# The attention's weights split during the first MLP, kept in DRAM, and a new order in the weight queue

## The chip, the cores and the metric

The kernel runs on one core of one Trainium2 chip. A core has five engines that work side by side, each through its own list of instructions in order: TensorE (PE in the profile) multiplies matrices, VectorE (DVE), ScalarE (ACT) and GpSimd (POOL) work element by element, and SyncE (SP) issues the transfers between DRAM and the on-chip memory SBUF. TensorE writes its sums into PSUM, from which DVE and ACT read them. An engine that waits for another one's result holds up everything behind it in its own list.

The metric is the device time of one execution in microseconds (us), the median of several runs.

## The reference, cut to what matters

The model has two layers over 512 tokens of 1024 numbers. The first layer mixes tokens with pooled averages; the second is a causal "stick-breaking" attention with 16 heads. Each is followed by an MLP with 4096 hidden values and a squared ReLU, and everything stands between root-mean-square norms.

```python
def sq_relu_mlp(h, w_up, w_down):
    u = jnp.matmul(h, w_up)
    return jnp.matmul(jnp.square(jax.nn.relu(u)), w_down)

for layer in range(DEPTH):
    h = rms_norm(x, mix_pre_g[layer])
    if layer < N_A:
        m = pool_mixer(h, pool_w[layer], pool_scale[layer])
    else:
        q = jnp.matmul(h, w_q[j])...
        o = stick_breaking_attention(q, k, v)
        m = jnp.matmul(o..., w_o[j])
    x = x + rms_norm(m, mix_post_g[layer])
    h = rms_norm(x, mlp_pre_g[layer])
    x = x + rms_norm(sq_relu_mlp(h, w_up[layer], w_down[layer]), mlp_post_g[layer])
    if layer == N_A - 1:
        kv = jnp.matmul(rms_norm(x, kv_norm_g), w_kv)
```

Inputs and output are float32. The gains of the norms ahead of the key, value and query projections can be multiplied into the weights' rows.

## The kernel before

**Products in three parts.** Every float32 product is made of three matmuls of a shorter type, fp32r. Each operand is split into a high part (a cast on ACT) and a low part (the rest after subtracting the high part, on DVE); the product is high x high + high x low + low x high. `mm3` (L217 to L219) and `up_block` (L555 to L557) issue such triples. `split` (L196, L197) does the two steps for activations, `weight` (L115) for weights: it loads a raw weight of 128x1024 numbers (512 KB) into one of two raw buffers, multiplies gains into it on POOL where the weight has any (two instructions at L138), casts it (L126) and subtracts (L128). Four of the first MLP's weights are subtracted on POOL, all others on DVE.

**The weight queue.** `queue` lists all weights that are split whole, in the order of use: for each layer the 32 column blocks of the up matrix (`up`) and the last four row blocks of the down matrix (`dn`), and ahead of the second layer's the 32 weights of the attention (8 `v`, 8 `k`, 8 `q` with gains, 8 `o` without). `fill` takes weights off its head as long as fewer than four are made and not yet used, `get` takes one out for use. The split weights lie in four slots, each with a high and a low tile. The `dn` weights have a place of their own (`dn_pool`), which exists only towards the end of an MLP, when buffers of the groups come free; `fill` stops at a `dn` weight until then. The first attention weights stand behind the four `dn` weights of the first MLP.

**The MLP.** 28 of the 32 hidden blocks are worked in five groups (of 2, 3, 3, 3 and 3 pairs) by a scheme that replaces eight block products by seven (class `Seven`). A group has seven products, each with a left operand (tile `a`, sums of squared activations, made on POOL at L417 and split at L196, L197) and a right operand (tile `w`, sums of blocks of the down matrix, made on DVE at L436 and split). The two halves of a group's down rows are loaded at L401, the second half into the tile `xn`. The operands are made two products ahead. Between the products stand the up products of the next group: 24 matmuls each, then ReLU and square on ACT. A product and an up product make one period. The first group starts when the first four up products are done. TensorE's part of a product is at L462, and its result is added to the tiles `y` at L471. After the groups, the last four hidden blocks are contracted plainly with the `dn` weights (`contract`); there the output's norm (`Update`: squares at L200, gains at L242, statistics at L206 and L213, the residual at L248, the next norm at L280) and its transposes for the next stage (L289) run along.

**Attention.** Sixteen heads in eight pairs run through a pipeline written out by hand (`ATT_ORDER`): values (V), keys and queries (K, P), scores and weights (S), transposes (T), mixing (A), output projections (O, E). `fill` is called in between.

**What sets the order.** The program text gives an order, and a scheduler that estimates when each instruction could run moves instructions within each engine's list, SP's among them, before the kernel is built. On the chip each list is then worked strictly in order. Buffers are named by tags: a new tile of a tag waits until the old tile's last reader is done. `grow` and `spare` are two such buffers of 512 KB, which hold rows of gains.

Of the kernel before, what the change touches and what calls it, by code (L numbers as in the profile page):

```python
# [10 lines left out]
F32 = mybir.dt.float32  # L11
# [4 lines left out]
P = 128  # L16
D = 1024
# [47 lines left out]
def trunk(ctx, tc, x, consts, gcol, grow, pw, wup, wdn, wq, wk, wv, wo, out):  # L65
# [3 lines left out]
    work = pool("work")  # L69
    wts = pool("wts")  # L70
    psum = pool("psum", 8, space=bass.MemoryType.PSUM)

    nc.scalar.preload_act_table_set("sigmoid_and_others")

# [74 lines left out]
    def place(k):  # L149

        if k[0] == "dn":
            return dn_pool[0].pop(0)
        if k == ("o", 6):
            both = att_pool[0].tile([P, 2, D], F32R, tag="v", bufs=2, name=name("w"))
            return [both[:, 0], both[:, 1]]
        if k == ("o", 7):
            return [att_pool[0].tile([P, NSEG], F32R, tag="w", bufs=2, name=name(x))[:, :D] for x in "hl"]
        return [wts.tile([P, D], F32R, tag=f"w{x}", bufs=4, name=name(x)) for x in "hl"]
# [314 lines left out]
    def mlp(l, mp, update):  # L473
# [46 lines left out]
        for g, group in enumerate(groups):  # L520
            coming = groups[g + 1] if g + 1 < len(groups) else None
            if coming:
                coming.squares()
            ups = list(range(firsts[g + 1], firsts[g + 1] + 2 * GROUPS[g + 1]) if coming else range(plain, NJ))
            for i in range(7):
                group.product(i, y, written if g == 0 else None)
                if i + 2 < 7:
                    if ups:
                        up(ups.pop(0))
# [5 lines left out]
                else:  # L535
# [4 lines left out]
                    elif i == 5:  # L540
                        piece = lambda tag, k, bufs=1: mp.tile([P, k, D], F32R, tag=tag, bufs=bufs, name=name("dn"))
                        w, e, x, z = piece("w1", 3), piece("e", 1), piece("w", 3, 2), piece("w", 3, 2)
                        dn_pool[0] = [
                            [w[:, 0], w[:, 1]], [w[:, 2], e[:, 0]], [x[:, 0], x[:, 1]], [x[:, 2], z[:, 0]],
                        ]
        w = [get(("dn", l, j)) for j in range(plain, NJ)]
# [101 lines left out]


    with tc.tile_pool(name="mlp0", bufs=1, reuse_waits="tile") as mp:  # L650
        gpost0 = gain_row(R_MLP_POST0)

        mlp(0, mp, lambda t, y: Update(t, gpost0, y, mlp_eps[t]))


    with tc.tile_pool(name="att", bufs=1, reuse_waits="tile") as ap:
# [197 lines left out]


    with tc.tile_pool(name="mlp1", bufs=1, reuse_waits="tile") as mp:
        gpost2 = gain_row(R_MLP_POST1)

        mlp(1, mp, lambda t, y: Update(t, gpost2, y, mlp_eps[t], final=True))


def constants():
# [49 lines left out]
```

## Time and profile before

| | us |
|---|---|
| median of 3 runs | 1006.39 (1005.23 to 1007.84) |
| the profiled execution | 1007.02 |
| its span, first to last instruction | 1005.1 |
| TensorE busy | 954.9 |
| DVE busy | 740.9 |
| ACT busy | 529.0 |
| POOL busy | 232.1 |

All rows come from one profiled execution. An instruction's row has its start, its duration, engine, line of the kernel, operation and tiles (output<-inputs); a bracket behind it says how long its engine had been idle and what it waited for. A row of a group has count, busy time and mean duration in ns, then the idle time before the group's instructions. A row of a window has its length, then the busy time of PE, PEld (TensorE's weight load), DVE, ACT and POOL with their counts, the granted share of TensorE's clock, the busy share of the transfer engines and their rate in GB/s; a window asked for one line alone has that line's engine only. A row of transfers has count, size and the median time from issue to landing.

### The profile page before, as it was taken

The numbers are of one execution on the slowest core, as the hardware profiler recorded it, in microseconds if no ns is written. First come the engines' busy times: TensorE is split into PE (matmuls) and PEld (weight loads), VectorE is DVE, ScalarE is ACT, GpSimd is POOL, SyncE is SP. The second block draws the span as 40 slices with busy tenths as digits, with TensorE's granted clock in tenths as the row PEclk, the third lists the DMA queues.
The fourth block names the chain that finished last, engine by engine and source line by source line (L and its number), as shares of the span: only waits on it lengthen the run. The fifth ranks groups of instructions, "written<-read, shape, count | busy, mean of one in ns | idle before, by whom it ended". The sixth has DMA issues, their size and how long they took to land.

```text
span 1005.1 us, 12276 instructions
## 1 busy us (share of the span) xinstructions
PE 954.9 (95%) x4823; PEld 812.2 (81%) x4823; DVE 740.9 (74%) x771; ACT 529.0 (53%) x837; POOL 232.1 (23%) x166
## 2 busy tenths in 40 slices
PE   7889999999999995999998999989999999999996
PEld 6888888888888884888787988788888888888885
DVE  5975595876858657489778989976587685957856
ACT  5655454444544536466656767557454444444532
POOL 1622040310203029132251300432040120303003
PEclk8999999999999997999999999999999999999998
DMA  7152513333141122122121211243423315133002
GB/s 265 65 185 86 188 42 126 105 126 105 63 137 73 43 63 63 52 75 64 56 70 54 73 64 64 84 147 103 138 95 126 126 42 188 25 135 114 8 34 84
DMA packets 26409, 94.45 MB, mean 94 GB/s; under 512 B 2544, under 2 KB 2928, under 8 KB 26352
## 3 DMA queue, kind: packets, MB, share of 16 engines
q1 hardware_dynamic: 26352, 93.67, 27.6%
q8 instruction: 38, 0.62, 0.3%
q14 instruction: 19, 0.16, 0.0%
HBM read 91.57 MB, written 2.10 MB: 93 GB/s over the span
## 4 chain that ended last, share of the span: by engine, by line
PE 81%; DVE 8%; ACT 4%; POOL 3%; DMA 2%; issue 2%; SPq 0%; POOLq 0%; DVEq 0%; ACTq 0%
PE ps L462 27%; PE ps L556 13%; PE ps L557 13%; PE ps L555 13%; PE ps L217 3%; PE ps L218 3%; PE ps L219 3%; PE ps L801 1%; DVE l L128 1%; DVE e L773 1%; POOL y L242 1%; ACT h L126 1%; PE ps L791 1%; PE ps L289 1%; PE ps L759 1%
## 5 line engine op out<-in xcount | busy, mean ns | idle before, releaser
L462 PE MATMUL ps<-w,a 128*128 128x512 f32 x1176 | 279.1, 390 | 4.5 <-ACT a L196 4.5
L556 PE MATMUL ps<-xnl,h 128*128 128x512 f32 (+1 forms) x712 | 262.9, 370 | 3.4 <-DVE xnl L197 3.4
L557 PE MATMUL ps<-xnh,l 128*128 128x512 f32 (+1 forms) x712 | 262.9, 370 | 0.5 <-DVE l L128 0.5
L462 PEld LDWEIGHTS ps<-w,a 128*128 128x128 f32 x1176 | 221.1, 188 | 50.7 <-ACT a L196 4.9
L555 PE MATMUL ps<-xnh,h 128*128 128x512 f32 (+1 forms) x712 | 261.7, 370 | 0.0
L128 DVE TENSOR_TENSOR l<-raw,h 128x1024 fp32r<-128x1024 f32 x93 | 123.0, 1323 | 78.3 <-ACT h L126 78.0
L126 ACT CAST h<-raw 128x1024 fp32r<-128x1024 f32 x97 | 102.1, 1054 | 142.8 <-PE ps L556 118.2
L556 PEld LDWEIGHTS ps<-xnl,h 128*128 128x128 f32 x712 | 135.5, 190 | 25.6 <-DVE xnl L197 3.6
L557 PEld LDWEIGHTS ps<-xnh,l 128*128 128x128 f32 x712 | 135.3, 190 | 23.1 <-DVE l L128 0.7
L555 PEld LDWEIGHTS ps<-xnh,h 128*128 128x128 f32 x712 | 134.8, 190 | 22.2
L471 DVE TENSOR_TENSOR y<-ps,y 128x512 f32<-128x512 f32 x124 | 84.7, 687 | 60.5 <-PE ps L462 60.3
L417 POOL TENSOR_TENSOR s<-r 128x768 f32<-128x768 f32 (+1 forms) x10 | 22.1, 2209 | 388.7 <-ACT r L493 388.7
L138 POOL TENSOR_TENSOR raw<-raw,gc 128x512 f32<-128x512 f32 x48 | 66.2, 1401 | 165.6 <-DMA raw<-in_wv 91.5
L196 ACT CAST a<-r 128x768 fp32r<-128x768 f32 (+1 forms) x60 | 47.7, 796 | 101.3 <-PE ps L462 64.0
L197 DVE TENSOR_TENSOR a<-r,a 128x768 fp32r<-128x768 f32 (+1 forms) x60 | 63.4, 1057 | 12.1 <-ACT a L196 12.1
L197 DVE TENSOR_TENSOR w<-e,w 128x1536 fp32r<-128x1536 f32 (+1 forms) x30 | 64.2, 2140 | 10.6 <-ACT w L196 10.1
L196 ACT CAST w<-e 128x1536 fp32r<-128x1536 f32 (+1 forms) x30 | 42.0, 1399 | 40.2 <-DVE e L436 27.6
L773 DVE TENSOR_TENSOR_SCAN e<-u,begin 128x1280 f32<-128x1280 f32 x16 | 47.5, 2971 | 7.8 <-ACT u L767 7.6
L417 POOL TENSOR_TENSOR r<-r 128x768 f32<-128x768 f32 (+1 forms) x20 | 42.6, 2128 | 39.7 <-DVE a L197 38.9
L242 POOL TENSOR_TENSOR y<-y,grow 128x512 f32<-128x512 f32 x12 | 21.1, 1761 | 114.0 <-ACT xn L200 114.0
L197 DVE TENSOR_TENSOR w<-w,w 128x1536 fp32r<-128x1536 f32 (+1 forms) x20 | 33.0, 1649 | 8.8 <-ACT w L196 8.8
L217 PE MATMUL ps<-h,xnh 128*128 128x256 f32 x128 | 36.6, 286 | 1.7 <-DVE kl L715 1.4
(131 smaller groups left out, 1481.0 us busy)
## 6 DMA issues: line engine op xcount, KB each, us to landing
raw<-in_wup SPq DMA_DIRECT2D x64, 512.0 KB, 3.5
w<-in_wdn SPq DMA_DIRECT2D x8, 1536.0 KB, 6.5
xn<-in_wdn SPq DMA_DIRECT2D x8, 1536.0 KB, 6.6
raw<-in_wdn SPq DMA_DIRECT2D x8, 512.0 KB, 3.9
raw<-in_wv SPq DMA_DIRECT2D x8, 512.0 KB, 3.5
raw<-in_wk SPq DMA_DIRECT2D x8, 512.0 KB, 3.5
raw<-in_wq SPq DMA_DIRECT2D x8, 512.0 KB, 3.5
raw<-in_wo SPq DMA_DIRECT2D x8, 512.0 KB, 3.6
```

Of the source, the lines that this page charges most:

```text
L126: nc.scalar.copy(hi, raw)
L128: on.tensor_tensor(out=lo, in0=raw, in1=hi.bitcast(F32), op=ALU.subtract)
L138: nc.gpsimd.tensor_tensor(out=v[:, h], in0=v[:, h], in1=g[:, h].broadcast_to((P, n // 2, D // n)), op=ALU.mult)
L196: latest["act"] = nc.scalar.copy(hi, src)
L197: latest["dve"] = nc.vector.tensor_tensor(out=lo, in0=src, in1=hi.bitcast(F32), op=ALU.subtract)
L217: nc.tensor.matmul(dst, ah, bh, start=start, stop=False)
L417: sub = lambda out, x, y, op=ALU.subtract: nc.gpsimd.tensor_tensor(out=out, in0=x, in1=y, op=op)
L462: nc.tensor.matmul(bank, a[:, x, q, TS[t]], w[:, z, q], start=start and q == 0 and k == 0, stop=q == self.n - 1 and k == 2, skip_group_che ...
L471: nc.vector.tensor_tensor(out=part, in0=bank, in1=part, op=ALU.add)
L555: nc.tensor.matmul(pu[:, cols], wh[:, k, :], xnh[:, k, cols], start=k == 0, stop=False)
L556: nc.tensor.matmul(pu[:, cols], wh[:, k, :], xnl[:, k, cols], start=False, stop=False)
L557: nc.tensor.matmul(pu[:, cols], wl[:, k, :], xnh[:, k, cols], start=False, stop=k == KC - 1)
```

## The change

A new function `split_apart` is called after each product of the first MLP's groups (twice at the fourth product of the second and third group). Each call loads one attention weight into a buffer of its own, scales it on POOL where it has gains, casts it on ACT and subtracts on DVE. Two pairs of buffers take turns, one new, the other made of `spare` and `grow`. Two weights are under way; with the third, the high and low part of the oldest are stored to DRAM (tiles `kept`) by two transfers. `make` then loads both parts of a weight that is kept straight into its slot, by two transfers, instead of calling `weight`.

```diff
+    apart, kept, going = [], {}, []
+
+    def split_apart(mp):
+        if len(going) > 1 or not apart and going:
+            k, parts = going.pop(0)
+            kept[k] = dram.tile([2, P, D], F32, tag=f"kept{len(kept)}", name=name("kept"))
+            for n in range(2):
+                nc.sync.dma_start(kept[k][n], parts[n].bitcast(F32))
+        if not apart:
+            return
+        k, src, scaled = apart.pop(0)
+        if len(apart) % 2:
+            raw = mp.tile([P, D], F32, tag="apart0", name=name("apart"))
+            hi = mp.tile([P, D], F32R, tag="apart1", name=name("apart"))
+        else:
+            raw = spare_tile()
+            hi = work.tile([P, D], F32R, tag="grow", name=name("apart"))
+        nc.sync.dma_start(raw, src)
+        if scaled is not None:
+            scaled(raw)
+        nc.scalar.copy(hi, raw)
+        nc.vector.tensor_tensor(out=raw, in0=raw, in1=hi.bitcast(F32), op=ALU.subtract)
+        going.append((k, (hi, raw)))
 
     def make():
         k, src, scaled = queue.pop(0)
+        if k in kept:
+            made[k] = place(k)
+            for n, t in enumerate(made[k]):
+                nc.sync.dma_start(t.bitcast(F32), kept[k][n])
+            return
```

In the queue, the attention's first four weights change places with the first MLP's four `dn` weights. One up product of the first group's row moves ahead of its first product, in both MLPs. The row of post gains is loaded behind the groups instead of ahead of the MLP, since its buffer is used by the splits. The high and low tile of a slot become one tile.

```diff
         if l == 1:
+            n = len(queue)
...
+            apart.extend(queue[n:])
+
+            queue[n - GRP : n + GRP] = queue[n : n + GRP] + queue[n - GRP : n]
...
+            if g == 0:
+                up(ups.pop(0))
             for i in range(7):
                 group.product(i, y, written if g == 0 else None)
+                if l == 0:
+                    for _ in range(2 if i == 3 and g in (1, 2) else 1):
+                        split_apart(mp)
...
+        gpost = gain_row((R_MLP_POST0, R_MLP_POST1)[l])
         w = [get(("dn", l, j)) for j in range(plain, NJ)]
         dn_pool[0] = None
         fill(ahead)
-        contract(squares[1:], w, y, False, update)
+        contract(squares[1:], w, y, False, lambda t, y: update(t, y, gpost))
```

More of the change, by code (lines that the diff above doesn't have):

```diff
@@ L71, in trunk @@
     psum = pool("psum", 8, space=bass.MemoryType.PSUM)
+    dram = pool("dram", space=bass.MemoryType.DRAM)
     nc.scalar.preload_act_table_set("sigmoid_and_others")
@@ L545, in mlp @@
                         ]
+        assert not apart and not going
+        gpost = gain_row((R_MLP_POST0, R_MLP_POST1)[l])
         w = [get(("dn", l, j)) for j in range(plain, NJ)]
@@ L650, in trunk @@
     with tc.tile_pool(name="mlp0", bufs=1, reuse_waits="tile") as mp:
-        gpost0 = gain_row(R_MLP_POST0)
-        mlp(0, mp, lambda t, y: Update(t, gpost0, y, mlp_eps[t]))
+        mlp(0, mp, lambda t, y, gpost: Update(t, gpost, y, mlp_eps[t]))
     with tc.tile_pool(name="att", bufs=1, reuse_waits="tile") as ap:
@@ L856, in trunk @@
     with tc.tile_pool(name="mlp1", bufs=1, reuse_waits="tile") as mp:
-        gpost2 = gain_row(R_MLP_POST1)
-        mlp(1, mp, lambda t, y: Update(t, gpost2, y, mlp_eps[t], final=True))
+        mlp(1, mp, lambda t, y, gpost: Update(t, gpost, y, mlp_eps[t], final=True))
 def constants():
```

7 lines of the change are left out of this document (4 added, 3 removed).

## The prediction

> **What bounds the kernel now.** I read the page first, then the busy time of each engine by stage, then TensorE's waits. The stages are cut where TensorE's groups of lines change: first MLP from 70, its end at 381, attention to 650, second MLP from 690.
>
> ```profile
> span 1005.1 us, 12276 instructions
> ...
> PE 954.9 (95%) x4823; PEld 812.2 (81%) x4823; DVE 740.9 (74%) x771; ACT 529.0 (53%) x837; POOL 232.1 (23%) x166
> ```
> ```profile
> core 0: us, PE busy (x) PEld busy (x) DVE busy (x) ACT busy (x) POOL busy (x), PEclk, DMA share, GB/s
> ...
> 70.00:90.00 20.00, 16.64 (x65) 13.48 (x64) 12.04 (x11) 12.91 (x21) 6.00 (x4) 0.83 0.25 79
> 90.00:312.00 222.00, 222.00 (x982) 183.80 (x981) 159.41 (x138) 107.41 (x125) 32.32 (x13) 1.00 0.33 112
> ...
> 190.00:251.00 61.00, 61.00 (x270) 50.49 (x269) 44.98 (x38) 28.82 (x32) 10.97 (x5) 1.00 0.30 104
> ...
> 381.00:402.00 21.00, 9.84 (x52) 8.45 (x51) 15.81 (x24) 12.88 (x31) 19.29 (x31) 0.67 0.16 50
> 402.00:650.00 248.00, 238.65 (x1388) 208.74 (x1388) 202.04 (x217) 156.45 (x316) 62.73 (x45) 0.99 0.21 66
> 650.00:690.00 40.00, 34.46 (x245) 32.30 (x245) 30.45 (x46) 24.90 (x46) 11.53 (x10) 0.96 0.35 120
> 690.00:985.00 295.00, 295.00 (x1303) 244.24 (x1303) 205.62 (x180) 139.64 (x165) 47.61 (x20) 1.00 0.27 93
> ```
> ```profile
> PE ps L217 <- DVE kl L715: 2.0, 2, 1.4
> PE ps L801 <- ACT ah L196: 1.7, 1, 1.7
> ```
>
> TensorE is the bound: 50.2 us of the span are left to it. In both MLPs it has no idle time (222.00 of 222, 295.00 of 295). What can be won lies in four places: the first MLP's start (3.36 idle), its end (11.16), attention (9.35) and the passage to the second MLP (5.54). The last two rows are the largest of ten pairs of lines on which TensorE waits in attention: many short waits. Each idle spell is followed by half clock: 0.83 over 20 us is 6.8 us at half rate, at most 3.4 lost.
>
> **The change, part by part.** The first MLP takes over 32 splits: 32 loads, 48 POOL scalings (24 weights), 32 casts, 32 subtractions, and 64 stores. Attention loses the same scalings, casts and subtractions, and its 32 loads become 64.
>
> *The first MLP's end.* The wait of 11.2 us ends with a norm (L280) that waits for POOL:
>
> ```profile
> 381.57 0.39 PE L219 MATMUL ps<-dn,sq 128*128 128x512 f32 x1
> 393.12 1.97 PE L289 MATMUL ps<-ident,xn 128*128 128x128 f32 x8 [11.16 <-ACT xn L280]
> ...
> 372.79 4.04 POOL L138 TENSOR_TENSOR raw<-raw,gc 128x512 f32<-128x512 f32 x4 [5.74 <-DMA raw<-in_wv]
> 376.79 3.99 POOL L242 TENSOR_TENSOR y<-y,grow 128x512 f32<-128x512 f32 x2
> ...
> 392.35 1.33 ACT L280 ACTIVATE xn<-x,stat 128x512 f32<-128x512 f32 x2 [1.07 <-POOL stat L213]
> ```
> ```profile
> L138 POOL TENSOR_TENSOR raw<-raw,gc 128x512 f32<-128x512 f32 x7 | 8.2, 1200 | 0.0
> ...
> L248 DVE SCALAR_TENSOR_TENSOR x<-y,stat,x 128x512 f32<-128x512 f32 x6 | 6.4, 1109 | 0.0
> L128 DVE TENSOR_TENSOR l<-raw,h 128x1024 fp32r<-128x1024 f32 x3 | 4.7, 1564 | 0.0
> ```
>
> The second fence groups 374 to 392. POOL scales attention's first weights (L138, 8.2 us) between the steps of the residual update, and DVE subtracts them (4.7). Both go. Of the two engines POOL stands last in the chain: its L242 could start at 374.8 instead of 376.8, and later links lose the rest of its 8.2. Upper end: all 11.2 and the slow clock behind it, about 13. Lower end 5 (DVE's 4.7 alone). DVE still has to do the second tile's L248 pair (2 x 1.1) ahead of the first tile's statistics, so a wait of some 2 us stays: I take 9. The four weights that now stand ahead of the down weights in the queue come from DRAM, so they cost no engine anything there.
>
> *The first MLP's start.*
>
> ```profile
> 74.25 1.22 PE L462 MATMUL ps<-w,a 128*128 128x512 f32 x2 [3.36 <-ACT a L196]
> ...
> 260.30 0.39 PE L556 MATMUL ps<-xnl,h 128*128 128x512 f32 x1
> 260.53 0.39 PE L557 MATMUL ps<-xnh,l 128*128 128x512 f32 x1
> ```
>
> An up product now stands ahead of the first product. It is 24 matmuls that start every 0.23 us, 5.4 us, and covers the 3.36; the cast that is waited for at 74.25 is done by 76.2. I take 5.4 of the 6.8 that idle time and slow clock make; lower end 2, since in the changed program's order a split's cast and subtraction stand ahead of this product's operands. The second MLP gets the same; its start belongs to the 5.54 below. Two products without an up product between them now end the first group, in both MLPs. The order puts the next group's first up product behind two of its matmuls, so the last splits stay covered; without that cover a weight cast and subtraction (1.5 and 1.75) would show: nothing taken, 3 us at worst in each.
>
> *Attention.* What leaves its engines:
>
> ```profile
> 402.00:650.00 248.00, 52.72 (x36) 0.99 0.21 66
> ...
> L128 DVE TENSOR_TENSOR l<-raw,h 128x1024 fp32r<-128x1024 f32 x29 | 38.7, 1339 | 8.5 <-ACT h L126 8.4
> ...
> 402.00:650.00 248.00, 31.64 (x30) 0.99 0.21 66
> ```
>
> From 402 to 650 these are POOL's L138 in the first row, DVE's L128 in the second, ACT's L126 in the third. DVE falls from 202 busy to some 165 of 248, ACT from 156 to 126, POOL to 10. TensorE waits here for splits of scores, keys and queries that queue on these engines. Ceiling: 9.35 idle, up to 2.5 of slow clock, and somewhat more, since a matmul's span (0.39) hides 0.16 of each gap; floor 2, if the waits are latency. I take 9. A weight's slot is now filled by two transfers (some 5 us, between the 3.5 and 6.6 below) where it took cast and subtraction (2.4): 2.6 later, hidden by four slots and 31 us for a pair of heads; each one exposed costs 2.6. The passage to the second MLP loses the last output weights' splits from DVE (30.45 of 40 busy): 4 of its 5.54 plus slow clock; ends 0 and 7. The post gain's load (4.9) moves behind the groups, ahead of its use by over 20 us: nothing.
>
> *What the first MLP pays.* TensorE cannot gain there. DVE has 44.98 of 61 us in a group (190 to 251), and the heaviest group gets eight splits, all scaled by POOL.
>
> ```profile
> L138 POOL TENSOR_TENSOR raw<-raw,gc x48: 1036/1042/3556, 365.0 to 576.6; 128x512 f32<-128x512 f32 x48
> ...
> 238.69 1.22 DVE L128 TENSOR_TENSOR l<-raw,h 128x1024 fp32r<-128x1024 f32 x1 [2.25 <-ACT h L126]
> ...
> 245.59 1.75 DVE L197 TENSOR_TENSOR w<-w,w 128x1536 fp32r<-128x1536 f32 x1
> ...
> 261.14 3.46 DVE L197 TENSOR_TENSOR w<-e,w 128x1536 fp32r<-128x1536 f32 x1
> ...
> 261.14 1.86 POOL L417 TENSOR_TENSOR r<-r 128x768 f32<-128x768 f32 x1 [4.03 <-DVE a L197]
> ...
> 255.92 2.00 DVE L197 TENSOR_TENSOR a<-r,a 128x768 fp32r<-128x768 f32 x1
> ...
> 260.75 1.07 PE L462 MATMUL ps<-w,a 128*128 128x512 f32 x4
> ```
>
> Eight subtractions of 1.22 make 54.8 of 61. Eight scalings of 2 x 1.042 are 16.7 us of POOL; the same DVE split takes 3.46 beside a POOL operation of 1.86 and 1.75 alone, so at worst DVE is stretched by all 16.7: 71.5, 10.5 over. Some of DVE's work reads PSUM and half of the meetings delay POOL (L138's 3556 at most): about 6 us, 60.8 of 61, just full. The margin is thinnest at a group's second product: its operand is done at 257.9 and used at 260.75. The Trainium skill, "SBUF — State Buffer", section "Who interferes with whom", says that a DVE operation with two SBUF inputs and a GpSimd operation that reads SBUF exclude each other for the whole instruction, whoever is first. The 3.46 agrees; by it the 10.5 over are the case in which POOL always comes first.
>
> The transfers:
>
> ```profile
> raw<-in_wv SPq DMA_DIRECT2D x8, 512.0 KB, 3.5
> ...
> xn<-in_wdn SPq DMA_DIRECT2D x8, 1536.0 KB, 6.6
> ...
> grow<-in_grow SPq DMA_DIRECT2D x4, 512.0 KB, 4.9
> ...
> out<-x SPq DMA_DIRECT2D x7, 256.0 KB, 2.0
> ...
> 10.00:20.00 10.00, 9.06 (x60) 8.94 (x60) 7.55 (x15) 4.04 (x6) 0.24 (x1) 0.73 0.88 344
> ```
>
> 30 of 32 splits fall into 90 to 312: 1.57 MB each, 47 MB, 213 GB/s on top of 112. That is 325 of some 390 (344 at a share of 0.88), so transfers queue. One buffer's round is load 3.5, scaling 2.1 to 2.8, cast 1.05, subtraction 1.2 to 2, store (no row of this size; 2.0 to 3.5, taken 3.2) and two issues of 0.33: 12.4 without a queue. Two are under way, so the round may last 61/8 x 2 = 15.3 us; in the first group, where nine splits stand in some 62 us, 13.8. A queue of 1 us at each transfer still fits; the second weights' load (6.6), on which a group's first operands wait, comes later by as much. The queue of SP holds 96 more issues, 32 us of 236; a store that waits for its subtraction holds up the up weights' loads behind it, which run three up products (28 us) ahead. A scaling that waits for its load holds up POOL's L417 behind it. ACT has room: 107 busy of 222 and 31 more.
>
> I take 7 us for this MLP: 3 where the first group ends, 3 around the group of eight, 1 in the next. Ends 0 and 25. Behind a subtraction that waits on DVE stand the operand splits of the next product, and TensorE behind those.
>
> Sum: the profiled execution took 1007.0 (span 1005.1 and 1.9 around it). 1007.0 - 5.4 - 9 - 9 - 4 + 7 = 986.6; the median of the runs is 0.6 lower: **986**.
>
> **Rivals.** (1) *Slower: the round of a split sets the first MLP's pace.* All engines hold these steps in program order, so a round of C us makes 32 splits last 16 C, where TensorE takes 236 us (76 to 312), C = 14.75. With 3 us of queue at each of the two transfers C is 18.4: +58, 1007 - 27 + 58 = 1038. It decides above C = 16.5, where the 27 us are used up. For it: 325 GB/s. Against it: idle engines in a group's second half, and six output weights of the last group without scaling. (2) *POOL's lock costs DVE most of the scalings*: 10.5 in the group of eight, some 5 in each of two others, 21 in all: 1001. (3) *Attention's waits are latency*: only start and end gain: 1007 - 14.4 - 2 + 7 = 998. For it: ten pairs of lines, none over 2.0 us. Against it: DVE's 202 of 248. (4) *The kept copies aren't used*: the changed order shows all 32 pairs loaded from them, so hardly.
>
> **How the numbers follow.** Forecast 0.50 (its own range 972 to 996), rival 1 0.22, rival 2 0.14, rival 3 0.13, rival 4 0.01. A difference under 0.3%, 3 us, can't be told from none. Faster: forecast, rivals 2 and 3 less a few hundredths: 0.73; same 0.05; slower 0.22. The ceilings of all four places give 963, with nothing paid; the range starts at 969 and ends at 1013, where the larger part of rival 1 is left out.
>
> **What would show it.** Right: no wait over 4 us at the end of the first MLP; DVE's L128 gone from attention and its idle time with TensorE under 4 us; in the first MLP's groups DVE near 60 of 61 and TensorE idle 3 to 10 us. Wrong: groups of 70 us or more with DVE or ACT waiting for POOL or a load (rival 1); L417 and L197 stretched with DVE always busy (rival 2); attention as long as before (rival 3).

## The result, and the profile after

| | us |
|---|---|
| before, median of 14 runs beside the changed kernel | 1006.08 (1001.30 to 1007.87) |
| after, median of 14 runs | 1009.61 (1007.07 to 1012.62) |
| ratio after / before | 1.0041, 95% interval 1.0027 to 1.0055 |
| predicted | 986 (969 to 1013) |

The changed kernel is slower by 0.4%. The time lies in the predicted range, but faster was forecast. Most lines below the new functions moved by 37: TensorE's product is L499 now (L462 before), the operand splits L233 and L234 (L196, L197), the weight split L127 and L129, a scaling L139, the norm L317, the transposes L326. New are the steps of a split apart: load L181, cast L184, subtraction L185, store L171, and the load of a kept copy L193.

The head of the page of after, the span and the engines' busy times:

```profile
span 1008.4 us, 12461 instructions
...
PE 957.0 (95%) x4823; PEld 812.1 (81%) x4823; DVE 744.5 (74%) x771; ACT 521.7 (52%) x837; POOL 248.6 (25%) x166
```

The engines have nearly as much work as before, as they should: the change moves work. So I divided both executions at three instants that mean the same in both: the first product, the first matmul with a `dn` weight, and the second MLP's first product. Busy times by stretch, before:

```profile
74.25:358.70 284.45, 284.45 (x1243) 235.26 (x1244) 203.29 (x176) 138.97 (x164) 46.41 (x20) 0.99 0.29 98
358.70:687.90 329.20, 303.15 (x1772) 266.21 (x1770) 259.94 (x298) 201.00 (x403) 103.80 (x93) 0.97 0.23 74
687.90:1005.10 317.20, 307.80 (x1368) 255.15 (x1368) 223.00 (x209) 146.64 (x184) 56.76 (x28) 0.99 0.27 93
```

and after, where attention and the way out of it, two parts of the second stretch, have rows of their own:

```profile
74.50:387.70 313.20, 289.22 (x1220) 234.54 (x1219) 255.01 (x205) 161.94 (x192) 119.81 (x63) 0.95 0.71 253
...
423.00:657.00 234.00, 233.76 (x1394) 208.22 (x1393) 161.46 (x192) 131.89 (x292) 11.07 (x14) 1.00 0.37 133
657.00:696.80 39.80, 36.13 (x258) 33.24 (x258) 28.91 (x45) 24.18 (x43) 11.80 (x10) 1.00 0.38 128
387.70:696.80 309.10, 301.28 (x1795) 267.48 (x1794) 211.06 (x268) 172.24 (x373) 35.79 (x46) 0.99 0.34 121
696.80:1008.40 311.60, 302.25 (x1345) 250.65 (x1343) 220.17 (x206) 141.93 (x181) 60.37 (x28) 0.99 0.28 94
```

From the `dn` weights on, the rest of the program takes 1008.4 - 387.7 = 620.7 us where it took 1005.1 - 358.7 = 646.4: 25.7 less. (An up product has moved across each of these instants, 23 matmuls in the counts, so only the sum of the second and third stretch is compared.) In attention TensorE now idles 0.24 us of 234, at full clock. Everything that the change was to bring there came. It was lost in the first MLP, which takes 28.8 us longer although it has 23 matmuls fewer. TensorE's waits in that stretch, in all, times, longest; before it had none but the 3.4 at the start:

```profile
PE ps L499 <- DVE w L234: 12.1, 4, 5.3
PE ps L499 <- ACT w L233: 9.4, 2, 7.6
PE ps L499 <- DVE a L234: 2.4, 3, 1.0
```

TensorE waits for the operands of its products, at the ends of the groups. The longest stop, in the timeline of all engines at the end of the first group (start, duration, instruction; the bracket is the idle time before it):

```profile
117.04 2.98 POOL L139 TENSOR_TENSOR apart<-apart,gc 128x512 f32<-128x512 f32 x2 [9.39 <-DVE a L234]
120.06 1.05 ACT L184 CAST apart<-apart 128x1024 fp32r<-128x1024 f32 x1 [4.48 <-POOL apart L139]
121.14 1.23 DVE L185 TENSOR_TENSOR apart<-apart,apart 128x1024 f32<-128x1024 f32 x1 [3.01 <-ACT apart L184]
122.45 2.04 POOL L139 TENSOR_TENSOR spare<-spare,gc 128x512 f32<-128x512 f32 x2 [2.42 <-DVE apart L185]
124.52 1.04 ACT L184 CAST apart<-spare 128x1024 fp32r<-128x1024 f32 x1 [3.41 <-POOL spare L139]
125.47 0.59 ACT L529 ACTIVATE r<-ps 128x512 f32<-128x512 f32 x1
...
128.15 1.47 ACT L233 CAST w<-w 128x1536 fp32r<-128x1536 f32 x1
...
129.67 1.22 PE L499 MATMUL ps<-w,a 128*128 128x512 f32 x2 [7.60 <-ACT w L233]
...
132.81 3.23 POOL L454 TENSOR_TENSOR r<-s,r 128x768 f32<-128x768 f32 x1
...
134.27 3.39 DVE L234 TENSOR_TENSOR w<-w,w 128x1536 fp32r<-128x1536 f32 x1
```

Two things are to be seen. First, ACT stands idle for 4.48 and 3.41 us at two casts of splits, with the ReLU of an up product and the operand cast of 128.15 behind them in its list; TensorE waits for that operand. Second, the subtraction at 134.27 takes 3.39 us beside a POOL operation of 3.23, where 1.75 is its time alone; that POOL operation is one of the MLP's own sums, not a scaling. The stop where the second group ends is all waiting: POOL waits for a split's load, DVE for the split's cast, and the operand's subtraction then takes its 1.75 alone.

```profile
190.81 2.08 POOL L139 TENSOR_TENSOR apart<-apart,gc 128x512 f32<-128x512 f32 x2 [6.43 <-DMA apart<-in_wk]
...
194.01 1.22 DVE L185 TENSOR_TENSOR apart<-apart,apart 128x1024 f32<-128x1024 f32 x1 [2.41 <-ACT apart L184]
...
199.27 1.75 DVE L234 TENSOR_TENSOR w<-w,w 128x1536 fp32r<-128x1536 f32 x1
...
201.07 6.79 PE L499 MATMUL ps<-w,a 128*128 128x512 f32 x16 [3.88 <-DVE w L234]
```

Waiting in order, or stretching: the experiments have to weigh them.

### The profile page after: what moved, and what is told of

The parts are those of the page before. It is cut to its first block, busy times and chain, and to the rows that moved or that the text cites. A ratio compares the mean times of both kernels' runs of the same rounds, so it can differ in the third digit from the quotient of the medians.

```text
span 1008.4 us, 12461 instructions
## 1 busy us (share of the span) xinstructions
PE 957.0 (95%) x4823; PEld 812.1 (81%) x4823; DVE 744.5 (74%) x771; ACT 521.7 (52%) x837; POOL 248.6 (25%) x166
## 4 chain that ended last, share of the span: by engine, by line
PE 61%; DVE 14%; DMA 12%; POOL 5%; issue 4%; ACT 3%; SPq 0%; POOLq 0%; DVEq 0%; ACTq 0%
PE ps L499 17%; PE ps L599 10%; PE ps L601 10%; PE ps L600 10%; DMA kept<-apart 5%; PE ps L254 3%; PE ps L255 3%; PE ps L256 3%; PE ps L843 2%; DVE x L285 2%; PE ps L833 2%; POOL apart L139 2%; DVE w L129 2%; DMA apart<-in_wk 2%; DMA kept<-spare 1%
## 5 line engine op out<-in xcount | busy, mean ns | idle before, releaser
L499 PE MATMUL ps<-w,a 128*128 128x512 f32 x1176 | 287.7, 398 | 24.0 <-DVE w L234 12.1
L499 PEld LDWEIGHTS ps<-w,a 128*128 128x128 f32 x1176 | 224.9, 192 | 76.1 <-DVE w L234 14.7
L600 PE MATMUL ps<-xnl,w 128*128 128x512 f32 (+1 forms) x712 | 262.4, 369 | 1.1 <-DVE xnl L234 1.1
L601 PE MATMUL ps<-xnh,w 128*128 128x512 f32 (+1 forms) x712 | 262.2, 369 | 0.0
L599 PE MATMUL ps<-xnh,w 128*128 128x512 f32 (+1 forms) x712 | 261.4, 370 | 0.0
L600 PEld LDWEIGHTS ps<-xnl,w 128*128 128x128 f32 x712 | 134.8, 189 | 23.3 <-DVE xnl L234 1.3
L601 PEld LDWEIGHTS ps<-xnh,w 128*128 128x128 f32 x712 | 134.8, 189 | 22.5
L599 PEld LDWEIGHTS ps<-xnh,w 128*128 128x128 f32 x712 | 134.2, 189 | 22.1
L129 DVE TENSOR_TENSOR w<-raw,w 128x1024 fp32r<-128x1024 f32 x62 | 83.8, 1355 | 36.7 <-ACT w L127 36.6
L279 POOL TENSOR_TENSOR y<-y,grow 128x512 f32<-128x512 f32 x12 | 17.9, 1493 | 319.6 <-ACT xn L237 319.6
L233 ACT CAST a<-r 128x768 fp32r<-128x768 f32 (+1 forms) x60 | 47.5, 793 | 59.0 <-PE ps L499 25.4
L233 ACT CAST w<-e 128x1536 fp32r<-128x1536 f32 (+1 forms) x30 | 41.9, 1395 | 57.8 <-DVE e L473 51.8
L127 ACT CAST w<-raw 128x1024 fp32r<-128x1024 f32 x66 | 68.7, 1042 | 3.4 <-DMA raw<-in_wup 3.0
L234 DVE TENSOR_TENSOR a<-r,a 128x768 fp32r<-128x768 f32 (+1 forms) x60 | 67.0, 1118 | 4.1 <-ACT a L233 4.0
L529 ACT ACTIVATE r<-ps 128x512 f32<-128x512 f32 x56 | 33.2, 593 | 67.4 <-PE ps L601 67.3
L454 POOL TENSOR_TENSOR r<-r 128x768 f32<-128x768 f32 (+1 forms) x20 | 53.1, 2653 | 45.0 <-DVE a L234 44.3
L234 DVE TENSOR_TENSOR w<-e,w 128x1536 fp32r<-128x1536 f32 (+1 forms) x30 | 55.8, 1860 | 4.0 <-ACT w L233 3.7
L815 DVE TENSOR_TENSOR_SCAN e<-u,begin 128x1280 f32<-128x1280 f32 x16 | 45.1, 2820 | 13.2 <-ACT u L809 13.0
L139 POOL TENSOR_TENSOR spare<-spare,gc 128x512 f32<-128x512 f32 x24 | 36.3, 1531 | 66.0 <-DMA spare<-in_wq 37.4
L139 POOL TENSOR_TENSOR apart<-apart,gc 128x512 f32<-128x512 f32 x24 | 39.2, 1652 | 33.2 <-DMA apart<-in_wk 20.5
```

The lines of the kernel that those rows point to most:

```text
L127: nc.scalar.copy(hi, raw)
L129: on.tensor_tensor(out=lo, in0=raw, in1=hi.bitcast(F32), op=ALU.subtract)
L139: nc.gpsimd.tensor_tensor(out=v[:, h], in0=v[:, h], in1=g[:, h].broadcast_to((P, n // 2, D // n)), op=ALU.mult)
L233: latest["act"] = nc.scalar.copy(hi, src)
L234: latest["dve"] = nc.vector.tensor_tensor(out=lo, in0=src, in1=hi.bitcast(F32), op=ALU.subtract)
L454: sub = lambda out, x, y, op=ALU.subtract: nc.gpsimd.tensor_tensor(out=out, in0=x, in1=y, op=op)
```

## The experiments

With the up products moved ahead and nothing else (`up_alone`, below), the first MLP's stretch has the same 1220 matmuls as after and TensorE is busy in all of its 276.0 us. So a stretch less 276.0 is what the splits cost there: 313.2 - 276.0 = 37.2 in the changed kernel, where 7 were predicted. Of these, 24.0 are TensorE's idle time (313.20 - 289.22), and 13.2 are the same matmuls taking longer (289.22 against 276.00) at a granted clock of 0.95. Each stretch comes from one execution, which lies up to 3.6 us below its run's median (scale_beside) and up to 4.3 above (half16, act16); where that matters, the medians stand beside it. The expectations speak of "loss", the sum of the delays between matmuls; those they give (9.7, 41.0, 15.1 and 13.1 for the first MLP) are within 0.4 us of the stretches' (10.1, 41.3, 15.3 and 13.5). The theories, by letter: A, the round of a split with its stores and transfers sets the pace; B, POOL's scalings cost VectorE its time; C, the order of the up products makes a stop by itself; D, the steps stand too early in the engines' lists; E, a chain of three steps is too long, whichever engines work it; F, D for what B leaves.

| run | median us | ratio to before (interval) | first MLP's stretch | DVE busy in it | POOL busy in it |
|---|---|---|---|---|---|
| up_alone | 999.4 | 0.9934 (0.9918, 0.9949) | 276.0 | 201.7 | 50.5 |
| neither | 982.8 | 0.9761 (0.9744, 0.9777) | 283.0 | 236.1 | 47.8 |
| no_scaling | 987.1 | 0.9810 (0.9789, 0.9831) | 286.1 | 235.2 | 53.9 |
| on_act | 990.8 | 0.9844 (0.9829, 0.9859) | 291.3 | 234.3 | 48.2 |
| act_pin | 994.5 | 0.9894 (0.9876, 0.9912) | 296.2 | 234.4 | 44.3 |
| scale_beside | 1005.6 | 0.9988 (0.9976, 0.9999) | 303.2 | 260.5 | 135.7 |
| one_store | 1006.4 | 1.0004 (0.9991, 1.0016) | 307.0 | 262.8 | 123.4 |
| after | 1009.6 | 1.0041 (1.0027, 1.0055) | 313.2 | 255.0 | 119.8 |
| pinned32 | 1013.5 | 1.0063 (1.0045, 1.0080) | 317.3 | 256.0 | 134.4 |

The runs above split all 32 weights (up_alone none). Those that split fewer are half16, light16, act16 and light4.

**The up products alone** (`up_alone`): the kernel before with one line pair of the change.

```diff
+            if g == 0:
+                up(ups.pop(0))
             for i in range(7):
                 group.product(i, y, written if g == 0 else None)
```

> The kernel before with one part alone: in both MLPs one up product moves ahead of the first group's first product. If that part is harmless: the wait at the first MLP's start and its slow clock go (6 us), no new stop in either MLP, 1000 to 1001. Theory C (two products without an up product between them leave the next group's operands uncovered): a stop of 3 us or more where the second group begins, in both MLPs, and a time of 1004 to 1008.

It took 999.4 us. Its stretch:

```profile
75.00:351.00 276.00, 276.00 (x1220) 228.60 (x1219) 201.74 (x174) 137.61 (x162) 50.53 (x20) 1.00 0.30 99
```

No idle time, none where the first group ends either: theory C falls. This edit alone brings 7 us (1006.5 - 999.4).

**The stores taken away** (`one_store`): only the first weight is stored, and the attention loads copies of it, as many bytes as before.

```diff
-            kept[k] = dram.tile([2, P, D], F32, tag=f"kept{len(kept)}", name=name("kept"))
-            for n in range(2):
-                nc.sync.dma_start(kept[k][n], parts[n].bitcast(F32))
+            if kept:
+                kept[k] = next(iter(kept.values()))
+            else:
+                kept[k] = dram.tile([2, P, D], F32, tag="kept0", name=name("kept"))
+                for n in range(2):
+                    nc.sync.dma_start(kept[k][n], parts[n].bitcast(F32))
```

> The changed kernel with the stores left out but for the first weight: both parts of that one are stored, and the attention loads these two tiles for every weight. Loads, scalings, casts and subtractions in the first MLP stay. Theory A (the round of a split sets the pace: a buffer waits for its stores, and the transfer engines are full where a group ends): the round falls from 18 us to about 13, TensorE's idle time between 70 and 352 falls from 24 us to under 8, and the time to 985 to 992. Theory B (POOL's scalings stretch DVE until it is full): nothing of that changes, idle time over 18 us, time over 1003.

```profile
76.20:383.20 307.00, 287.09 (x1220) 231.93 (x1220) 262.79 (x206) 162.45 (x192) 123.44 (x62) 0.97 0.47 158
```

The transfer engines' share falls from 0.71 to 0.47, and the scalings wait for their loads 34.7 us in place of 75.5 (between 75 and 350). Yet of the 37.2 us only 6.2 go (3.2 by the medians, 1009.6 - 1006.4), and TensorE's idle time of 19.9 us (307.00 - 287.09) is what theory B expected. Theory A falls as the main cause.

**The gains left out of the splits** (`no_scaling`): POOL gets none of the 48 scalings, and the kept weights lack their gains.

```diff
-        if scaled is not None:
-            scaled(raw)
         nc.scalar.copy(hi, raw)
```

> The changed kernel with the gains left out of the splits: POOL scales nothing in the first MLP. Theory A: the round is shorter by the scaling alone, 18 to about 15.5, the stops at the groups' ends shrink but don't go: 8 to 16 us idle, 993 to 1002. Theory B: DVE is no longer stretched, under 4 us idle, 985 to 989.

```profile
77.00:363.10 286.10, 279.60 (x1221) 229.49 (x1220) 235.16 (x203) 159.97 (x190) 53.89 (x19) 0.99 0.76 275
```

With loads, casts, subtractions and stores all there, and the transfers as dense as in after (0.76), 10.1 us are left of 37.2; the medians differ by 22.5 (1009.6 - 987.1). VectorE works 235.2 us in place of 255.0 on as many instructions (203 and 205). Theory B stands, though 6.5 us of idle time (286.10 - 279.60) are left where it expected under 4; but this edit also takes a step out of each split's chain.

**POOL's work put beside the chain** (`scale_beside`): 48 POOL operations of the same size, into a scratch tile. The gains are left out here too. The split's own cast and subtraction do not wait for these operations; only the next cast into that high tile does.

```diff
-        if scaled is not None:
-            scaled(raw)
         nc.scalar.copy(hi, raw)
+        if scaled is not None:
+            for h in NS:
+                beside = mp.tile([P, 512], F32, tag="beside", name=name("beside"))
+                nc.gpsimd.tensor_tensor(out=beside, in0=hi[:, h].bitcast(F32), in1=hi[:, h].bitcast(F32), op=ALU.mult)
```

> The changed kernel with 48 POOL operations of the same shape in the first MLP that multiply the high part into a scratch tile after the cast, in place of the gains: POOL and its port are as busy as before, but neither cast nor subtraction waits for POOL. Theory D: as without scalings, 984 to 991. Theory B: as the changed kernel, 1003 to 1012.

```profile
77.30:380.50 303.20, 283.61 (x1219) 232.33 (x1218) 260.45 (x204) 161.46 (x191) 135.74 (x64) 0.97 0.74 261
```

17.1 us of the 27.1 come back (18.5 of 22.5 by the medians; the profiled execution is the fastest of the ten), and VectorE's work is up by 25.3 (260.45 - 235.16) for one instruction more. In VectorE's waits of this run (75 to 350) the splits' casts hold it up for 15.4 us,

```profile
DVE spare L187 <- ACT apart L182: 10.9, 5, 3.8
...
DVE apart L187 <- ACT apart L182: 4.5, 4, 3.0
```

in after for 44.2:

```profile
DVE apart L185 <- ACT apart L184: 24.0, 9, 5.2
DVE spare L185 <- ACT apart L184: 20.2, 6, 4.9
```

So the larger part needs no chain: it is there when POOL merely works beside the split. That VectorE's stretch alone makes it is not shown, for POOL's own sums for the operands stand behind the added work too: of this run's three long stops (4.57, 4.69 and 8.14 us) the second ends with a cast that had waited 9.75 us for such a sum. The other 10 us of after (4.0 by the medians) stand beside 29 us more of waits in order. That these make them is not shown either: no_scaling has 29.4 us of such waits and pays 10.1 in all.

**The gains multiplied by ScalarE** (`on_act`): nothing is left out.

```diff
-            scaled(raw)
+            scaled(raw, True)
...
-        def scaled(raw):
+        def scaled(raw, on_act=False):
             v = raw.rearrange("p (k c) -> p k c", k=n)
+            if on_act:
+                for k in range(n):
+                    nc.scalar.activation(v[:, k], v[:, k], ACT.Copy, scale=gc[:, lo + k : lo + k + 1])
+                return
```

> The changed kernel with the gains of the split weights multiplied by ScalarE in place of POOL: 8 pieces of 128x128 for each key and query weight, 4 of 128x256 for each value weight, on the same tile before its cast. Nothing is left out. ScalarE gets about 8 x 0.35 = 2.8 us for each of 16 weights and 4 x 0.45 = 1.8 us for each of 8, some 59 us more of work in the first MLP (it was busy 173 of 286 us there without the gains), and the chain of a split is as long as before or longer. Theory B (the cost is POOL's work beside VectorE's): VectorE's work falls back to about 246 us in the first MLP, the loss of TensorE there to 10 to 16 us, time 987 to 994. Rival theory E (a chain of three steps in the engines' order makes them wait for each other, whichever engine has the first): the loss stays at 28 us or above, time 1004 to 1015.

```profile
77.50:368.80 291.30, 281.39 (x1219) 230.46 (x1218) 234.31 (x205) 204.84 (x334) 48.22 (x18) 0.99 0.77 271
```

It took 990.8 us, in theory B's interval, with a chain that is no shorter than after's, though with one hand-over between engines fewer: 15.3 us are paid in place of 37.2 (the medians differ by 18.8). VectorE does the same 205 instructions in 20.7 us less. ACT has 43 us more work, and VectorE does not feel it (234.3 and, without any scaling, 235.2). Theory E falls. This version beats the kernel before by 1.6%, and the changed one by 1.9% (990.8 / 1009.6).

**Neither gains nor stores** (`neither`): the edits of no_scaling and one_store together.

> The changed kernel without the gains of the split weights and without the stores but the first weight's; the attention loads copies of that one weight, as many bytes as before. The gains alone left 9.7 us of loss in the first MLP. If the stores and the transfers' queue make the rest (theory A for the rest), 3 to 5 us remain and the time is 980 to 983; if the casts and subtractions themselves make it, standing in ScalarE's and VectorE's order where a group ends, 8 to 10 us remain and the time is 985 to 988.

```profile
77.00:360.00 283.00, 279.06 (x1221) 229.64 (x1220) 236.10 (x203) 160.32 (x190) 47.83 (x19) 0.99 0.49 166
```

The median is theory A's, 4.4 us below no_scaling's; the stretch pays 7.0 in place of 10.1, more than the 3 to 5 expected. So the stores and their traffic make 3 us here and 6.2 with POOL at work (one_store), or 4.4 and 3.2 by the medians, and loads, casts and subtractions by themselves 7.0.

**Every second period** (`half16`): the first 16 weights, one call in every second period.

```diff
-            apart.extend(queue[n:])
+            apart.extend(queue[n : n + 16])
...
-                    for _ in range(2 if i == 3 and g in (1, 2) else 1):
+                    if (7 * g + i) % 2 == 0:
                         split_apart(mp)
```

> The changed kernel with half the splits at half the pace: the attention's first 16 weights, one in every second period, the other 16 as before in the attention. Theory A: a round may last 30 us, so under 3 us of idle time in the first MLP's groups; the start and the end keep their gains (13), attention keeps half of its own (5 to 7): 986 to 990. Theory B: each split still costs DVE its 1.2 and POOL's 2.1, some 8 us of idle time: 994 to 998.

It took 1006.3 us, ratio 1.0001 (0.9989 to 1.0013), longer than both theories expected. Its stretch, and from the timeline the end of the first group:

```profile
75.70:375.90 300.20, 284.57 (x1220) 232.32 (x1220) 229.29 (x189) 147.62 (x176) 84.72 (x43) 0.97 0.52 181
```
```profile
132.16 1.22 PE L499 MATMUL ps<-w,a 128*128 128x512 f32 x2 [9.14 <-ACT w L233]
```

The 16 loads were issued from 53 to 188 us, as densely as after's, since the scheduler moved the splits ahead as far as their buffers allow. So the pace in the program's text is not the pace in the lists, and the run could not test a slower one. It shows that the first 16 splits, as densely placed, cost 24.2 us by themselves, of which some 4 may be this execution's (the slowest of twelve, 4.3 above their median). The stop of 9.14 us holds no stretched scaling: two weights' scalings at 119.18 and 124.95 us take 2.04 each, behind waits of 10.78 and 3.73 for loads, and ACT waits for them 4.92 and 4.72, with the operand's cast behind in its list.

**All 32 held in place** (`pinned32`): the call stands behind the operand splits of its period, and each step is held behind the period's last operation on its engine.

```diff
-            scaled(raw)
-        nc.scalar.copy(hi, raw)
-        nc.vector.tensor_tensor(out=raw, in0=raw, in1=hi.bitcast(F32), op=ALU.subtract)
+            with tc.issue_after(latest["sub"].ins):
+                scaled(raw)
+        with tc.issue_after(latest["act"].ins):
+            nc.scalar.copy(hi, raw)
+        with tc.issue_after(latest["dve"].ins):
+            nc.vector.tensor_tensor(out=raw, in0=raw, in1=hi.bitcast(F32), op=ALU.subtract)
```

> The changed kernel with the same 32 splits at the same pace, but each split's scaling, cast and subtraction held behind the operand splits of its period on POOL, ACT and DVE (the scheduler had moved them ahead of these). Theory D (the steps stand too early in the lists: ACT and DVE stop at a step whose load comes later on the chip than the scheduler assumed, with the next operands behind it): TensorE's idle time between 70 and 352 falls from 24 us to under 8, the time to 984 to 991. Theory B (POOL's scalings block or stretch DVE, wherever they stand): idle time over 15 us, time over 1000.

```profile
77.00:394.30 317.30, 289.67 (x1220) 235.09 (x1219) 255.97 (x206) 164.20 (x194) 134.37 (x67) 0.95 0.74 258
```
```profile
346.30 6.04 PE L504 MATMUL ps<-w,a 128*128 128x512 f32 x16 [9.93 <-DVE w L237]
```

1013.5 us: later in the lists is not better. The stop of 7.6 at the first group's end shrinks to 2.5, but others appear, the longest of 9.93 in the last group. Theory D falls for the whole; for the stop at the first group's end it holds.

**Held, with the gains on ScalarE** (`act_pin`): the edits of pinned32 and on_act together.

> The kernel with the gains on ScalarE, and the steps of each split held behind the operand splits of their period on ScalarE and VectorE, as in the run that held all 32 in place. Nothing is left out. Theory B alone (POOL beside VectorE was the cost of the held version too): its loss of 41.0 us in the first MLP falls by the 22 us that the move to ScalarE saved in the changed kernel, to about 19, time 990 to 998. Theory F (what is left with the gains on ScalarE is the splits' steps run too early, where a group ends): the loss falls below the 15.1 us of the version that is not held, to 5 to 10, time 981 to 987.

```profile
75.00:371.20 296.20, 283.93 (x1220) 232.65 (x1219) 234.40 (x206) 214.15 (x354) 44.27 (x19) 0.97 0.79 277
```

The stretch falls by 21.1 us against pinned32 (VectorE's work by 21.6), as theory B expected, and is 4.9 longer than on_act's. Theory F falls. Moving the scalings off POOL is worth nearly the same in two quite different orders: 21.9 and 21.1 us, 18.8 and 19.0 by the medians.

**Half the weights, in quiet periods** (`light16`): pinned32 with the first 16 weights, behind products 1 to 4 of the first four groups.

```diff
-            apart.extend(queue[n:])
+            apart.extend(queue[n : n + 16])
...
+                if l == 0 and i in (1, 2, 3, 4):
+                    split_apart(mp)
```

> As pinned32, with the attention's first 16 weights alone, one each behind the second to fifth product of the first four groups, none where a group ends or begins; the other 16 are split in the attention as before. Theory D: no idle time over 3 us in the first MLP's groups, start and end keep 13 us, attention 5 to 7: 986 to 990. Theory B: some 8 us of idle time stay: 994 to 999.

```profile
76.00:365.50 289.50, 279.57 (x1221) 229.38 (x1220) 232.01 (x190) 149.67 (x178) 90.82 (x47) 0.99 0.56 196
```

996.8 us, ratio 0.9896 (0.9883 to 0.9909), in theory B's interval. But it pays 13.5 us here, against half16's 24.2 for the same weights (the medians are 9.5 apart), so where the splits stand is worth some 10 us with 16 of them, which no run with all 32 shows. From the `dn` weights on takes 995.8 - 365.5 = 630.3, about halfway between 620.7 with all splits gone and up_alone's 645.5 with none.

**The same with the gains on ScalarE** (`act16`).

> The kernel with only the first 16 weights split, held behind products 1 to 4 of the first four groups, with their gains on ScalarE; the other 16 are cast and subtracted in the attention as before. Nothing is left out. The same with the gains on POOL took 996.8 us and lost 13.1 us in the first MLP, 9.7 in the attention. Theory B: the first MLP's loss falls to 0 to 4 us, the attention's stays at 9 to 10, time 986 to 989. Theory E (the chain's length, whichever engine): the loss stays at 10 or above, time 995 to 999.

```profile
76.00:361.00 285.00, 279.42 (x1219) 230.19 (x1218) 223.11 (x190) 179.88 (x274) 47.02 (x19) 0.99 0.57 199
```

992.5 us, ratio 0.9875 (0.9855 to 0.9895), between the two theories' intervals. The stretch pays 9.0 in place of 13.5: theory B is right in direction (VectorE's work falls by 8.9), but I expected 0 to 4. The 28 scalings that leave POOL here (47 instructions against 19) are worth 4.5 us, 0.16 each, where the 48 of after are worth 21.9, 0.46 each: the price of one depends on where it stands. The profiled execution is the longest of the five (996.8; the others 991.5 to 994.1), so its 9.0 is likely too much. One stop of 3.95 us where the second group ends stays with POOL out of play, and what makes it is not settled.

**Four weights** (`light4`): light16 with four weights.

> As light16 with the first four weights alone, in the first group: what the start (6) and the end (7) of the first MLP bring without any gain in the attention. Both theories: 992 to 995; over 997 would say that the end's gain hangs on something else.

```profile
75.20:351.30 276.10, 276.10 (x1219) 228.49 (x1218) 208.19 (x178) 138.68 (x166) 59.48 (x27) 1.00 0.41 137
```

997.9 us, ratio 0.9908 (0.9888 to 0.9927): the first MLP pays nothing, but the time is over 997. The end of the first MLP is relieved as in after, its longest stop being 3.92 us in place of up_alone's 11.26. Yet from the `dn` weights on the run takes 642.7 us where up_alone takes 645.5, so only 2.8 of the 7 expected arrive: attention has a new wait of 2.8 us, and TensorE's busy time is 2.9 us longer (613.94 against 611.03, the clock being 0.98 in both). Why is not settled; the end's gain does hang on what follows.

## Why the prediction was wrong

By the first matmul with a `dn` weight the start had gained 7.7 us (358.7 before, 351.0 in up_alone), and the splits had cost 36.7 (387.7 in after); the rest of the program gained 25.7. That leaves the 3.3 us by which the span grew.

**The start (5.4 us): right, a little low.** up_alone shows 7 us, with both MLPs' starts in it. Of the fear that a split would stand ahead of the first products' operands, a wait of 0.8 us at 84.1 is left.

**The end of the first MLP, attention and the passage (9 + 9 + 4): right in the sum, a little low.** The profile gives 25.7 us for the 22; up_alone has 0.9 of them without any split. Point by point: the stop at the end fell from 11.16 to 3.92 us (no wait over 4, as said); TensorE's idle time in attention from 9.35 to 0.24, in the passage only from 5.54 to 3.67, with a clock of 1.00 in place of 0.96. The terms can't be weighed singly, as light4 shows for the end. VectorE's weight subtraction (L129) is gone from attention but for two instructions that already belong to the second MLP's weights (the last row below: VectorE's and POOL's time on that line). The 64 loads of kept copies cost nothing that can be seen. Rival 3, attention's waits as latency, is refuted: they went with the splits' work on DVE, ACT and POOL, behind which they had been queueing.

```profile
414.89 1.73 PE L326 MATMUL ps<-ident,xn 128*128 128x128 f32 x8 [3.92 <-ACT xn L317]
```
```profile
423.00:657.00 234.00, 2.36 (x2) 0.00 (x0) 1.00 0.37 133
```

**What the first MLP pays (7 us): the step that failed.** It was 37.2, beyond the upper end of 25. The prediction tried the group of eight splits by one sum: VectorE's work after a part of the stretch, "about 6 us, 60.8 of 61, just full", and took what is not full as free. Two things are wrong in it.

The first is the size. I counted the lock for one group of eight. It acts on all 48 scalings: VectorE's same instructions take 20 us longer with POOL (255.0 against 234.3 and 235.2), and POOL is stretched as well: (119.8 - 48.2) / 45 = 1.59 us for a scaling that takes 1.04 alone (45 of the 48 fall into the stretch, 63 instructions against 18). Half of each meeting to either side was a fair guess; the number of meetings was not. Rival 2 had this mechanism and put it at 21 us. Moving the scalings to ScalarE saves 21.9 in the stretch (18.8 by the medians), and leaving them out 27.1 (22.5); how much of that is VectorE's stretch, how much POOL's own late sums and how much waiting in order, the runs do not separate. The Trainium skill, "SBUF — State Buffer", section "Who interferes with whom", gives GpSimd no port of its own, only VectorE's second pair, and ScalarE its own ports. The runs agree: 48 scalings on POOL stretch VectorE by 20 us, the same scalings on ScalarE by none that can be seen. Where rows show a stretch, the operation has both inputs in SBUF, as the operands' subtraction here (2334 ns against 1749); the addition to `y`, which reads PSUM, has none (679 and 681). The rows are VectorE's between 75 and 350 us, of after and then of no_scaling, with count, busy time and mean ns:

```profile
L508 DVE TENSOR_TENSOR y<-ps,y 128x512 f32<-128x512 f32 x49 | 32.5, 679 | 0.0
...
L234 DVE TENSOR_TENSOR w<-w,w 128x1536 fp32r<-128x1536 f32 x7 | 16.3, 2334 | 0.0
```
```profile
L506 DVE TENSOR_TENSOR y<-ps,y 128x512 f32<-128x512 f32 x56 | 37.4, 681 | 6.1 <-PE ps L497 6.0
...
L232 DVE TENSOR_TENSOR w<-w,w 128x1536 fp32r<-128x1536 f32 x8 | 14.0, 1749 | 0.4 <-ACT w L231 0.4
```

The size alone would have cost nothing by the prediction's sum, in which VectorE's work is free until it fills the group.

The second is the measure, and here the sum itself failed. A group's mean says nothing about its end. Three stretches of after, about as long as the second to the fourth group, each with the end of the group ahead of it:

```profile
129.00:198.00 69.00, 65.62 (x273) 52.94 (x273) 57.45 (x45) 35.59 (x41) 26.80 (x14) 0.95 0.73 258
198.00:267.00 69.00, 64.46 (x267) 51.89 (x267) 58.16 (x45) 32.89 (x38) 37.71 (x20) 0.95 0.73 253
267.00:333.00 66.00, 59.76 (x252) 48.95 (x253) 57.77 (x49) 36.17 (x41) 18.08 (x8) 0.92 0.81 294
```

VectorE is busy 58 of 69, 58 of 69 and 58 of 66, far from full, and TensorE still idles 3.4, 4.5 and 6.2 us. The operands for the next group's first products are made in a few microseconds at its predecessor's end, with a lead of 3 us (done at 257.9, used at 260.75, as the prediction itself quoted); a stretched or waiting instruction there comes through to TensorE at once, with a clock of 0.92 to 0.95 behind it. Of the three places that I priced at 3, 3 and 1, the first alone has a stop of 7.60, and there are others of 3.88 and 5.27 at the next two group ends (201 and 274 us).

**Rival 1 (a split's round sets the pace, 1038)** had the right sign, and not the right cause. The issues of the loads into `spare` (tiles, count, durations in ns, first and last start):

```profile
L181 SPq DMA_DIRECT2D spare<-in_wq x8: 328/332/425, 66.0 to 271.4; - x8
...
L181 SPq DMA_DIRECT2D spare<-in_wv x4: 328/332/333, 52.2 to 252.0; - x4
...
L181 SPq DMA_DIRECT2D spare<-in_wo x4: 333/333/424, 158.4 to 318.9; - x4
```

16 loads from 52.2 to 318.9 make a round of 17.8 us, above the 16.5 from which it was to decide. But it is as long as two of TensorE's periods with their stops (313.2 / 35 x 2 = 17.9), so it says nothing of which follows which. one_store does: there the same loads start from 53.9 to 240.6, a round of 12.4 us, and 31.0 us are lost all the same. Theory A expected 985 to 992, and 1006.4 came out.

```profile
L184 SPq DMA_DIRECT2D spare<-in_wv x4: 327/328/328, 53.9 to 186.6; - x4
L184 SPq DMA_DIRECT2D spare<-in_wo x4: 328/328/328, 125.8 to 240.6; - x4
```

The prediction's signs could not have told rivals 1 and 2 apart: in after ACT waits for POOL's scalings for 72.3 us between 75 and 350, as the one says, and VectorE's operations are stretched, as the other says, though VectorE is not always busy. Rival 4 is refuted by the loads of kept copies.

**The chances.** Faster had 0.73. Together the gains came to more than forecast (33.4 us against 27.4); the loss hung on one line, for which the row of 3.46 us stood in the prediction, and I priced it for the heaviest group alone. That 1009.6 lies inside 969 to 1013 is luck: the upper end stood for a part of rival 1, whose cause was not at work. One sum has a slip: the ceilings as listed (6.8, 13, 9.35 + 2.5 and "somewhat more", 7) add up to 38.7 and give 968; 963 would need 5 us for the "somewhat more". What is open is why 7 us are left without gains and stores, and 9 with half the weights (act16): they fall at group ends, but no run took the casts or the subtractions away alone.

## What to carry to other kernels

Work moved under a stage that TensorE bounds is not free because each engine has idle time there on average: count the operations that meet on a shared resource over the whole stage, look at which steps an engine must wait for with other work behind them in its list, and look at the shortest lead between an operand and its use. A two-input operation on POOL beside a busy VectorE is paid by both; a per-partition scale belongs on ScalarE if that has room, which here turned 1.0041 into 0.9844. Try such a change in parts: the two cheapest (an up product moved ahead, four weights split early) brought 0.9%, 0.7% of it by the up product alone, with no cost in the first MLP, and the other 28 weights only another 0.6% even with the gains on ScalarE.

## What the runs showed of the hardware

ScalarE's work did not slow VectorE: with 45 us more of it than no_scaling (204.8 against 160.0) VectorE's work in the stretch was 234.3 us (235.2), while 66 us more of POOL's (119.8 against 53.9) made it 255.0. Transfers were cheaper than feared. In the first MLP, at 253 to 277 GB/s (shares of 0.71 to 0.79), the stores cost 3 to 6 us by the two runs without them; what the 32 loads cost there was not taken by itself. Attention idled 0.24 us with its 64 loads at 133 GB/s.

The prediction has half clock behind each idle spell. In after the clock was 1.00 behind the stops of 0.82 and 1.89 us (84.1 to 100 and 164 to 175 us), and 0.53, 0.55 and 0.59 in the 6 to 7 us behind those of 7.60, 3.88 and 5.27.
